# Three groups of small products in the first token mixer, written for the whole TensorE array

## The chip, the cores and the metric

The kernel runs on one core of one Trainium2 chip. The metric is device time in microseconds of one execution, as the median of several runs. Beside these runs there is one profiled execution, from which all durations below come.

## What is computed

The reference is a two-layer decoder trunk on 1024 tokens of width 1024. Layer 0 mixes tokens with RWKV-7, layer 1 with a gated DeltaNet; each is followed by a dense SwiGLU network, and by normalisations that a conditioning vector shifts and scales. Only the inner recurrence of the first mixer is touched by the change. Per head (16 heads of 64 channels) it is

```python
def step(S, inp):
    r_t, k_t, v_t, w_t, a_t, b_t = inp
    sa = jnp.einsum('bhvk,bhk->bhv', S, a_t)
    S = S * w_t[:, :, None, :] + sa[..., None] * b_t[:, :, None, :] + v_t[..., None] * k_t[:, :, None, :]
    return S, jnp.einsum('bhvk,bhk->bhv', S, r_t)
```

The kernel does this in chunks of 64 tokens: within a chunk the dependence of each step on the earlier ones is a triangular 64 by 64 system per head, whose inverse is computed with small products, and between chunks only the 64 by 64 state of each head is carried on.

## The kernel before

**Stages.** The program is written as generators that yield estimated costs, and a weaving loop (`weave`, `interleave`) that takes the next piece of whichever generator is behind. The projections of RWKV (`proj_rwkv`) come first. Then the mixer's 32 units (`pairs`: two heads, which lie in the two halves of the 128 partitions, by 256 tokens, that is four chunks) are woven with dense work: 19 of the 35 steps with the rest of the projections, the other 16 with the output projection of layer 0, its normalisation, the feed-forward of the first half of the tokens and the conditioning products of layer 1. This woven stretch goes from about 250 to 1350 us of the profile. After it come the gated DeltaNet and the rest of the dense work, in which the mixer has no part. Each engine has one queue and works it in order; what stands where in it is settled when the program is built, from the order of the code, its yields, and what each piece needs.

**A unit** has three parts.

- `prep1` makes the inputs of the four chunks. In it the scores of the two heads are computed: for each head four products of 64 rows (the head's 64 channels) by 128 columns, on one half of the array's rows (L1071), into a PSUM bank of the two under the name `p1`; then VectorE (DVE) masks them into `sa` and `sr` (L1072, L1073, whose helper has line L212) and the generator yields. The other head's four products and their two evictions follow.
- `prep2` calls `inverse` (L823 on). It works on four matrices of 128 by 128 at a time, each with two 64 by 64 blocks on its diagonal, in f16. Two of its products, the one that L895 starts (`nh` with `x`; here called the block product) and the last one, `fin` (L954: `r` with `xt`), are written as pairs of 64 by 64 products on the two diagonal quarters of the array, eight to a group. `r` comes from PSUM in one instruction on all 128 partitions: on ScalarE (ACT, L951) in the first 17 units and on DVE (L947, helper line L212) in the other 15. All products of `inverse` have line L836 and share the one PSUM bank `pa`.
- `chain` (L1112 on) carries the state through the four chunks. Per chunk: state times `ar` (L1127, 128 by 128), a subtraction-like addition on DVE (`w`), the inverse times `w` on one quarter of the array (L1136), a copy to `uv`, then the masked scores `sr` times `uv` (L1143), which add to half of the partitions of the bank `pc`, with 128 rows and 64 columns of the array, and the state's update (L1145, 128 by 128).

In the profile, the shape ahead of a matmul tells the part of the array that it uses, rows by columns: `64*128` for the scores, `64*64` for the quarters, `128*64` for L1143, `128*128` for the dense products of 512 columns (L264 to L266). A product in f32 is recorded as two matmuls, so the eight products of L1071 of a unit are 16 records and the two of L1143 in a chunk are four.

The mask of the two diagonal blocks, and the lines around the change:

```python
HALF = slice(0, 64), slice(64, P)
```

Of the kernel before, what the change touches and what calls it, by code (L numbers as in the profile page):

```python
# [10 lines left out]
F16 = mybir.dt.float16  # L11
# [4 lines left out]
ADD, SUB, MUL = ALU.add, ALU.subtract, ALU.mult  # L16

P = 128
# [39 lines left out]
def body(ctx, tc, A):  # L58
    nc = tc.nc
    pe, dve, act, pool, sync = nc.tensor, nc.vector, nc.scalar, nc.gpsimd, nc.sync  # L60
# [21 lines left out]
    def tl(pl, shape, dt, tag, bufs=1):  # L82
        return pl.tile(shape, dt, tag=tag, name=nm(tag), bufs=bufs)
# [33 lines left out]
    def p1_ps():  # L117
        return bank("p1")
# [24 lines left out]
    def C(n):  # L143
        o = COFF[n]
        return cst[:, o:o + dict(_CST)[n]]
# [65 lines left out]
    def tt(eng, out, a, b, op):  # L211
        eng.tensor_tensor(out=out, in0=a, in1=b, op=op)  # L212
# [587 lines left out]
    def setup(pl, nlev, sets):  # L800


        ms = [[tl(pl, [P, 4, P], F16, f"n{e}{q}") for e in "hl"] + [tl(pl, [P, 4, P], F16, f"nd{q}")] for q in range(2)]
        if nlev == 7:
            xt = tl(pl, [P, 4, P], F16, "xf")
        for q in range(2):
            if nlev == 7:
                ms[q].append(xt)
            for t in ms[q][3:] if nlev == 7 else ms[q][:2]:
                pool.memset(t[:, :, :], 0.0)  # L810
        zs = []
        for q in range(sets):
            zs.append([tl(pl, [P, 4, P], F16, f"z{q}{j}") for j in range(nlev - 2)])
            for z in zs[-1][:2]:
                pool.memset(z[:, :, :], 0.0)
            for z in zs[-1][2:]:
                for i in range(4):
                    act.copy(out=z[:, i, :], in_=C("ident"))
        return ms, zs

    HALF = slice(0, 64), slice(64, P)

    def inverse(pl, zs, m3, nlev, kn):  # L823


        SE, RM, FM = KN[kn]
        nh, nl, nd = m3[:3]

        def four(f, w=P):
            t = pa_ps()  # L830
            for i in range(4):
                f(t[:, w * i:w * i + w], i)
            return v3(t[:, 0:4 * w], 4)

        def one(out, l, r, start=True, stop=True):
            pe.matmul(out, l, r, start=start, stop=stop)  # L836
# [32 lines left out]
        x = series(zs[0], stack[:, 0:32].unsqueeze(1).to_broadcast([P, 4, 32]), "ix")  # L869
        xt = compact("iy")  # L870
        dve.transpose(flat(xt), flat(x))
        yield 2.0
        for m in (1, 2):
# [4 lines left out]
            if m == 1:  # L878
                xt = series(z, xt[:, :, :], "ixt")
                x = compact("iy")  # L880
# [8 lines left out]
        def half(f):  # L889
            def g(o, i):  # L890
                for R in HALF:
                    f(o[R, :], i, R)
            return g

        t = four(half(lambda o, i, R: one(o, nh[R, i, R], x[R, i, :])), 64)  # L895
        z = zs[3]
        for o in (0, 64):
            if 'z' in OP[0 if kn == 6 else 1] and o:
# [43 lines left out]
            xi = tl(pl, [P, 4, w], F16, "jxi", 1)  # L942
            tt(pool, xi[:, :, :], units, x[:, :, :], SUB)
        t = four(res, w)
        r = tl(pl, [P, 4, w], F16, "jr", 1)
        if RM == 2:
            tt(dve, r[:, :, :], t, xi[:, :, :], ADD)  # L947
        elif RM:
            tt(dve, r[:, :, :], t, units, ADD)
        else:  # L950
            act.copy(out=r[:, :, :], in_=t)  # L951
        yield 1.0

        def fin(o, i):  # L954
            if w == 64:
                for R in HALF:
                    one(o[R, :], r[R, i, :], xt[R, i, :], True, bool(FM))
            else:
                one(o, r[:, i, :], xt[:, i, :], True, bool(FM))
            if not FM:  # L960
                one(o, ident16[:, :], xt[:, i, :], False, True)

# [26 lines left out]
    def prep1(rp, nb, ctxr, h, p, q, n, box):  # L989
# [54 lines left out]
        def q4(t):  # L1044
            return t.rearrange("p (i q t) -> p i q t", i=2, q=4)
# [17 lines left out]
        yield 1.4  # L1063
        sr, sa = tl(rp, [P, 2, 2, 2, 64], F32, "sr", nb["sc"]), tl(rp, [P, 2, 2, 2, 64], F32, "sa", 1)
        inc, stc = (C("mske")[:, 64 * j:64 * j + 64].unsqueeze(1).unsqueeze(1).to_broadcast([P, 2, 2, 64]) for j in range(2))
        for hh in range(2):
            t = p1_ps()
            R = slice(64 * hh, 64 * hh + 64)
            for c in range(4):
                o = P * c  # L1070
                pe.matmul(t[:, o:o + P], bk[R, o:o + P], ar[R, o:o + P], start=True, stop=True)  # L1071
            tt(dve, sa[:, hh, :, :, :], q4(t)[:, :, 1:3, :], stc, MUL)  # L1072
            tt(dve, sr[:, hh, :, :, :], q4(t)[:, :, 0::3, :], inc, MUL)  # L1073
            yield 1.8
        m3 = ctxr[0][n % 2]
        nh, nl = m3[:2]
        for x, R in ((1, slice(0, 64)), (0, slice(64, P))):
# [34 lines left out]
    def chain(rp, nb, ctxr, h, p, q, box):  # L1112
# [7 lines left out]
        for c in range(4):  # L1120
            i, x = divmod(c, 2)
            rr, aa = (HS[0], HS[1]) if x == 0 else (HS[1], HS[0])
            np_ = tl(rp, [P, P], F32, "np", nb["np"])
            if 'n' not in OP[h]:
                act.activation(out=np_[:, :], in_=n0[:, :], func=AF.Copy, scale=dcol[:, c:c + 1])
            pq = pc_ps()
            pe.matmul(pq[:, 0:P], ar[:, P * c:P * c + P], n0[:, :], start=True, stop=True)  # L1127
            w = tl(rp, [P, P], F32, f"w{x}", 1)
            if 'w' in OP[h]:
                pe.matmul(pq[aa, 0:P], C("ident")[aa, aa], uv[aa, i, x, :], start=False, stop=True, skip_group_check=True)  # L1130
                act.copy(out=w[aa, :], in_=pq[aa, 0:P])
            else:
                tt(dve, w[aa, :], pq[aa, 0:P], uv[aa, i, x, :], ADD)
            yield 0.9
            for hs, hh in zip(HS, range(2)):
                pe.matmul(pq[aa, 128 + 64 * hh:192 + 64 * hh], tinv[aa, 2 * hh + i, :], w[aa, hs], start=True, stop=True)  # L1136
            if 'u' in OP[h]:
                act.copy(out=uv[aa, i, x, :], in_=pq[aa, P:2 * P])
            else:
                dve.tensor_copy(out=uv[aa, i, x, :], in_=pq[aa, P:2 * P])  # L1140
            yield 1.0
            for hs, hh in zip(HS, range(2)):
                pe.matmul(pq[rr, hs], sr[:, hh, i, x, :], uv[:, i, x, hs], start=False, stop=True, skip_group_check=True)  # L1143
            pst = pq[:, 2 * P:3 * P]
            pe.matmul(pst, bkn[:, c, :], uv[:, i, x, :], start=True, stop='n' not in OP[h])  # L1145
            if 'n' in OP[h]:
                pe.matmul(pst, C("ident"), n0[:, :], start=False, stop=True)
            for hs in HS:
                if 'n' in OP[h]:
                    if hs.start and 'N' in OP[h]:  # L1150
                        dve.tensor_scalar(out=n0[hs, hs], in0=pst[hs, hs], scalar1=dcol[hs, c:c + 1], scalar2=None, op0=MUL)
                    else:
                        act.activation(out=n0[hs, hs], in_=pst[hs, hs], func=AF.Copy, scale=dcol[hs, c:c + 1])
                    continue
                stt(n0[hs, hs], pst[hs, hs], dcol[hs, c:c + 1], np_[hs, hs], MUL, ADD)
            act.copy(out=yn[rr, P * i:P * i + P], in_=pq[rr, 0:P])
            yield 2.1
# [462 lines left out]
```

## Time and profile before

| what | value |
|---|---|
| median of 3 runs | 3382.88 us (3382.76 to 3385.67) |
| the profiled execution, as timed | 3386.16 us |
| its span, first to last instruction | 3384.4 us |
| mean granted TensorE clock | 0.972 |
| TensorE (PE) busy | 3222.6 us, 95% |
| DVE, ACT, POOL busy | 61%, 42%, 33% |
| window 250 to 1350 us: PE, DVE busy | 1056.94, 809.81 us |

In what follows a row of the view by groups reads: line, engine, operation, what it writes and reads, shapes, count, then the union of its busy time in us and the mean of one in ns, then idle time of its engine just before. A row of the view in order of time reads: start, duration (both us), engine, line, operation, count. The duration of a matmul in these rows reaches to its end in a pipeline, so neighbours overlap; what a matmul costs the queue is the step from its start to the start of the next.

### The profile page before, as it was taken

How to read it: one execution, taken by the hardware profiler on the slowest of the kernel's cores; microseconds unless marked ns; L12 is line 12 of the kernel's file. 1: busy time of each engine (PE TensorE's matmuls, PEld its weight loads, DVE VectorE, ACT ScalarE, POOL GpSimd, SP SyncE). 2: the span in 40 equal slices, each digit the busy share in tenths (PEclk: the TensorE clock that was granted, in tenths of full speed). 3: DMA queues.
4: the chain of work that ended last, by engine and by line, in shares of the span. 5: the costliest groups of instructions: out<-in, count | busy, mean ns of one | idle time of the engine just before them, and what ended most of it. 6: DMA issues, size and time to landing. Idle time of an engine off the chain costs nothing.

```text
span 3384.4 us, 52492 instructions
## 1 busy us (share of the span) xinstructions
PE 3222.6 (95%) x19408; PEld 2462.3 (73%) x19408; DVE 2074.1 (61%) x4534; ACT 1405.1 (42%) x2718; POOL 1129.7 (33%) x1353
## 2 busy tenths in 40 slices
PE   7989999998999999998999999999999999999997
PEld 4667777765776776676877777777777777878886
DVE  5556888887666666476476555575477653563235
ACT  4655677643333332355432232365432322342222
POOL 3553232344444443555521000220244444520001
PEclk8988999997999999999999999999999999999998
DMA  7773334352544454655654554566654446465553
GB/s 268 261 240 95 117 99 130 111 175 87 169 164 167 141 172 142 214 176 191 234 194 158 184 171 171 206 201 216 221 182 146 161 159 231 164 216 179 199 178 133
DMA packets 240529, 594.16 MB, mean 176 GB/s; under 512 B 24720, under 2 KB 80656, under 8 KB 240272
## 3 DMA queue, kind: packets, MB, share of 16 engines
q1 hardware_dynamic: 240128, 590.74, 51.8%
q8 instruction: 152, 2.49, 0.3%
q14 instruction: 105, 0.86, 0.1%
q10 hardware_dynamic: 144, 0.07, 0.0%
HBM read 440.04 MB, written 150.67 MB: 175 GB/s over the span
## 4 chain that ended last, share of the span: by engine, by line
PE 43%; DVE 4%; ACT 2%; DMA 2%; issue 2%; POOL 2%; SPq 0%; ACTq 0%; POOLq 0%; DVEq 0%
PE mm L264 13%; PE mm L265 12%; PE mm L266 12%; PE pa L836 1%; DVE e L215 1%; POOL wl L212 1%; PE p L1354 1%; DMA wr<-w_in 1%; ACT wh L222 1%; PE pc L1388 0%; PE pc L1392 0%; DMA yr<-y 0%; PE p L1336 0%; PE pc L1397 0%; PE pc L1399 0%
## 5 line engine op out<-in xcount | busy, mean ns | idle before, releaser
L264 PE MATMUL mm<-s,wh 128*128 128x512 f32 x2608 | 1079.0, 414 | 14.9 <-DVE e L215 5.5
L265 PE MATMUL mm<-s,wh 128*128 128x512 f32 x2608 | 1055.0, 405 | 11.7 <-POOL s L212 7.6
L266 PE MATMUL mm<-s,wl 128*128 128x512 f32 x2608 | 1047.8, 402 | 0.0
L212 POOL TENSOR_TENSOR wl<-wr,wh 128x256 fp32r<-128x256 f32 (+1 forms) x828 | 651.3, 817 | 876.7 <-ACT wh L222 829.4
L264 PEld LDWEIGHTS mm<-s,wh 128*128 128x128 f32 x2608 | 495.9, 190 | 132.6 <-issue 23.3
L265 PEld LDWEIGHTS mm<-s,wh 128*128 128x128 f32 x2608 | 497.2, 191 | 105.7 <-POOL s L212 12.2
L266 PEld LDWEIGHTS mm<-s,wl 128*128 128x128 f32 x2608 | 496.8, 191 | 94.8 <-POOL wl L212 0.3
L252 ACT CAST wh<-wr 128x1024 fp32r<-128x1024 f32 x199 | 206.8, 1049 | 497.8 <-PE mm L265 243.1
L222 ACT CAST wh<-wr 128x1024 fp32r<-128x1024 f32 (+1 forms) x254 | 228.4, 905 | 360.4 <-PE mm L265 196.8
L215 DVE SCALAR_TENSOR_TENSOR x<-mm,modp,x 128x512 f32<-128x512 f32 x272 | 202.3, 748 | 72.8 <-PE mm L266 70.9
L264 PE MATMUL mm<-ys,wh 128*128 128x512 f32 x544 | 219.1, 403 | 3.8 <-DVE x L215 3.8
L265 PE MATMUL mm<-ys,wh 128*128 128x512 f32 x544 | 216.9, 399 | 0.0
L266 PE MATMUL mm<-ys,wl 128*128 128x512 f32 x544 | 216.7, 398 | 0.0
L215 DVE SCALAR_TENSOR_TENSOR e<-e,vec,e 128x512 f32<-128x512 f32 x144 | 124.2, 866 | 97.2 <-ACT e L1300 89.9
L212 DVE TENSOR_TENSOR e<-mm,e 128x512 f32<-128x512 f32 x88 | 60.7, 690 | 165.2 <-PE mm L266 165.1
L836 PEld LDWEIGHTS <-z 128*128 128x128 f16 x1600 | 83.6, 97 | 100.7 <-issue 63.4
L215 DVE SCALAR_TENSOR_TENSOR e<-e,mm 128x512 f32<-128x512 f32 x88 | 60.2, 684 | 145.8 <-ACT e L679 145.5
L215 DVE SCALAR_TENSOR_TENSOR tx<-mm,modp,tx 128x512 f32<-128x512 f32 x112 | 83.1, 748 | 75.0 <-PE mm L266 73.3
L212 DVE TENSOR_TENSOR s<-e,s 128x512 fp32r<-128x512 f32 x106 | 84.1, 795 | 70.6 <-ACT s L222 70.3
L264 PEld LDWEIGHTS mm<-ys,wh 128*128 128x128 f32 x544 | 103.3, 190 | 30.5 <-DVE x L215 4.7
L266 PEld LDWEIGHTS mm<-ys,wl 128*128 128x128 f32 x544 | 103.2, 190 | 25.6
L265 PEld LDWEIGHTS mm<-ys,wh 128*128 128x128 f32 x544 | 103.4, 190 | 25.1 <-issue 0.5
(393 smaller groups left out, 5364.1 us busy)
## 6 DMA issues: line engine op xcount, KB each, us to landing
wr<-w_in SPq DMA_DIRECT2D x176, 512.0 KB, 4.5
ada<-ada_w SPq DMA_DIRECT2D x96, 512.0 KB, 5.3
loi<-wl SPq DMA_DIRECT2D x88, 512.0 KB, 2.9
wr<-w_ffo SPq DMA_DIRECT2D x88, 512.0 KB, 5.1
wl<-loi SPq DMA_DIRECT2D x88, 512.0 KB, 3.7
wr<-w_g SPq DMA_DIRECT2D x64, 512.0 KB, 4.6
lof<-wl SPq DMA_DIRECT2D x44, 512.0 KB, 2.9
wl<-lof SPq DMA_DIRECT2D x44, 512.0 KB, 3.5
```

Of the source, the lines that this page charges most:

```text
L212: eng.tensor_tensor(out=out, in0=a, in1=b, op=op)
L215: return dve.scalar_tensor_tensor(out=out, in0=a, scalar=s, in1=b, op0=op0, op1=op1)
L222: act.copy(out=hi, in_=src)
L252: act.copy(out=hi[:, :], in_=raw[:, :])
L264: pe.matmul(out, wh[:, off:off + P], ah, start=start, stop=False)
L265: pe.matmul(out, wh[:, off:off + P], al, start=False, stop=False)
L266: pe.matmul(out, wl[:, off:off + P], ah, start=False, stop=stop)
L836: pe.matmul(out, l, r, start=start, stop=stop)
L1354: pe.matmul(t[:, 256 * e:256 * e + 256], kq[:, c, 0, :], kq[:, c, :, :].rearrange("p a b -> p (a b)"), start=True, stop=True)
```

## The change

- **Scores.** Both heads' eight products are issued one after the other into two banks, then the four evictions follow, then one yield of the sum of the two earlier costs.
- **Inverse.** In the first mixer the block product and `fin` are done with four 128 by 128 products each instead of eight of 64 by 64. For this `fin` needs a left operand that is zero outside of the two diagonal blocks: a new tile `rf`, cleared once on POOL in `setup`, into whose blocks `r` is written in two instructions of 64 partitions each instead of one of 128. Of the gated DeltaNet's inverse no instruction changes.
- **Masked scores times values.** L1143 takes the scores of both chunks of the pair as its 128 columns and writes all 128 partitions of the bank, of which the half that is read is the same as before.

```diff
@@ setup
         if nlev == 7:
             xt = tl(pl, [P, 4, P], F16, "xf")
+        else:
+            rt = tl(pl, [P, 4, P], F16, "rf")
+            pool.memset(rt[:, :, :], 0.0)
         for q in range(2):
-            if nlev == 7:
-                ms[q].append(xt)
+            ms[q] += [xt if nlev == 7 else rt]
@@ inverse
-        t = four(half(lambda o, i, R: one(o, nh[R, i, R], x[R, i, :])), 64)
+        if nlev == 6:
+            t = four(lambda o, i: one(o, nh[:, i, :], x[:, i, :]), 64)
+        else:
+            t = four(half(lambda o, i, R: one(o, nh[R, i, R], x[R, i, :])), 64)
...
-        r = tl(pl, [P, 4, w], F16, "jr", 1)
-        if RM == 2:
-            tt(dve, r[:, :, :], t, xi[:, :, :], ADD)
...
-        else:
-            act.copy(out=r[:, :, :], in_=t)
+        r = m3[3] if w == 64 else tl(pl, [P, 4, w], F16, "jr", 1)
+        for R, cols in [(R, R) for R in HALF] if w == 64 else [(slice(0, P), slice(0, P))]:
+            if RM == 2:
+                tt(dve, r[R, :, cols], t[R, :, :], xi[R, :, :], ADD)
...
+            else:
+                act.copy(out=r[R, :, cols], in_=t[R, :, :])
         yield 1.0
 
         def fin(o, i):
-            if w == 64:
-                for R in HALF:
-                    one(o[R, :], r[R, i, :], xt[R, i, :], True, bool(FM))
-            else:
-                one(o, r[:, i, :], xt[:, i, :], True, bool(FM))
+            one(o, r[:, i, :], xt[:, i, :], True, bool(FM))
@@ prep1
+        both = p1_ps(), p1_ps()
         for hh in range(2):
-            t = p1_ps()
-            R = slice(64 * hh, 64 * hh + 64)
             for c in range(4):
-                o = P * c
-                pe.matmul(t[:, o:o + P], bk[R, o:o + P], ar[R, o:o + P], start=True, stop=True)
-            tt(dve, sa[:, hh, :, :, :], q4(t)[:, :, 1:3, :], stc, MUL)
-            tt(dve, sr[:, hh, :, :, :], q4(t)[:, :, 0::3, :], inc, MUL)
-            yield 1.8
+                o, R = P * c, HALF[hh]
+                pe.matmul(both[hh][:, o:o + P], bk[R, o:o + P], ar[R, o:o + P], start=True, stop=True)
+        for hh in range(2):
+            tt(dve, sa[:, hh, :, :, :], q4(both[hh])[:, :, 1:3, :], stc, MUL)
+            tt(dve, sr[:, hh, :, :, :], q4(both[hh])[:, :, 0::3, :], inc, MUL)
+        yield 3.6
@@ chain
-                pe.matmul(pq[rr, hs], sr[:, hh, i, x, :], uv[:, i, x, hs], start=False, stop=True, skip_group_check=True)
+                pe.matmul(pq[:, hs], sr[:, hh, i, :, :].rearrange("p x t -> p (x t)"), uv[:, i, x, hs], start=False, stop=True,
+                          skip_group_check=True)
```

The change also moves instructions in the queues. The first place is the scores of one unit early in the second half of the woven stretch, on PE. Before, the rows are (`p` is a scores bank, `z`, `nh` are matrices of the inverse; the last figures of a row are the partitions and elements written, and a number behind `x` counts equal rows):

```order
L836 LDWEIGHTS z_717_2344
L836 MATMUL pa_9580<-ixt_9481,z_717_2344 128x32
L1071 MATMUL p_2371_9540<-ar_9488,bk_9489 128x128 x4
L1136 MATMUL pc_9573<-w_2382_9575,ti_9311 64x64 x2
L1071 MATMUL p_2386_9593<-ar_9488,bk_9489 128x128 x4
L836 LDWEIGHTS nh_712_2335
L836 MATMUL pa_9612<-jx_9586,nh_712_2335 64x64
```

and now the same unit's scores stand like this (L1072 is L1071 of before, L1129 is L1127, L838 is L836):

```order
L265 MATMUL p_2345_9373<-l0l_2380,g2h_8543 128x256
L266 MATMUL p_2345_9373<-l0h_2379,g2l_8544 128x256
L1129 MATMUL pc_9449<-n_186_268,ar_8519 128x128
L1072 MATMUL p_2355_9406<-ar_9354,bk_9355 128x128 x4
L1072 MATMUL p_2356_9407<-ar_9354,bk_9355 128x128 x4
L838 LDWEIGHTS z_718_2346
L838 MATMUL pa_9453<-ixt_9347,z_718_2346 128x32
```

The two groups of four, which had a quarter-array product of another unit's chain between them, now stand together.

The second place is the end of a chunk in a chain, late in the stretch, also on PE, with the block product of another unit's inverse behind it. Before:

```order
L266 MATMUL mm_14898<-s_11009,wl_14890 128x512
L1143 MATMUL pc_14863<-uv_13909,sr_13798 64x64 x2
L1145 MATMUL pc_14863<-uv_13909,bkn_14022 128x128
L836 LDWEIGHTS nh_712_2335
L836 MATMUL pa_14917<-jx_14873,nh_712_2335 64x64
```

and now (L1145 is L1143 of before, L1148 is L1145):

```order
L266 MATMUL mm_14684<-s_10851,wl_14676 128x512
L1145 MATMUL pc_14656<-uv_13707,sr_13600 128x64 x2
L1148 MATMUL pc_14656<-uv_13707,bkn_13816 128x128
L838 LDWEIGHTS nh_712_2335
L838 MATMUL pa_14703<-jx_14666,nh_712_2335 128x64
```

The order is the same; the products of L1143 and of the block product write 128 partitions instead of 64, and the latter are four instead of eight. Behind the last product of the mixer PE's queue holds the same instructions in the same order as before.

More of the change, by code (lines that the diff above doesn't have):

```diff
@@ L944, in inverse @@
         t = four(res, w)
-        r = tl(pl, [P, 4, w], F16, "jr", 1)
-        if RM == 2:
-            tt(dve, r[:, :, :], t, xi[:, :, :], ADD)
-        elif RM:
-            tt(dve, r[:, :, :], t, units, ADD)
-        else:
-            act.copy(out=r[:, :, :], in_=t)
+        r = m3[3] if w == 64 else tl(pl, [P, 4, w], F16, "jr", 1)
+        for R, cols in [(R, R) for R in HALF] if w == 64 else [(slice(0, P), slice(0, P))]:
+            if RM == 2:
+                tt(dve, r[R, :, cols], t[R, :, :], xi[R, :, :], ADD)
+            elif RM:
+                tt(dve, r[R, :, cols], t[R, :, :], units[R, :, :], ADD)
+            else:
+                act.copy(out=r[R, :, cols], in_=t[R, :, :])
         yield 1.0
         def fin(o, i):
-            if w == 64:
-                for R in HALF:
-                    one(o[R, :], r[R, i, :], xt[R, i, :], True, bool(FM))
-            else:
-                one(o, r[:, i, :], xt[:, i, :], True, bool(FM))
+            one(o, r[:, i, :], xt[:, i, :], True, bool(FM))
             if not FM:
```

## The prediction

> **What bounds the kernel now.** I read the page first, for the share of each engine, then the busy times by window in the stretch where the mixer is woven with dense work, then who waited for whom there.
>
> ```profile
> span 3384.4 us, 52492 instructions
> PE 3222.6 (95%) x19408; PEld 2462.3 (73%) x19408; DVE 2074.1 (61%) x4534; ACT 1405.1 (42%) x2718; POOL 1129.7 (33%) x1353
> PE 43%; DVE 4%; ACT 2%; DMA 2%; issue 2%; POOL 2%; SPq 0%; ACTq 0%; POOLq 0%; DVEq 0%
> ```
>
> PE is the engine that is nearly always at work, and the chain that ended last lies mostly on it. By window of 50 us (length, then busy us of PE, weight loads, DVE, ACT, POOL, then the granted clock), with the sum over all 22 windows from 250 to 1350 us last:
>
> ```profile
> 400.00:450.00 50.00, 49.97 (x475) 37.55 (x472) 44.66 (x132) 36.52 (x98) 16.00 (x21) 1.00 0.38 118
> 550.00:600.00 50.00, 49.36 (x448) 37.08 (x447) 44.70 (x123) 38.69 (x99) 14.54 (x21) 1.00 0.48 149
> sum 1100.00, PE 1056.94 PEld 774.99 DVE 809.81 ACT 535.60 POOL 438.42; mean PE 48.04 PEld 35.23 DVE 36.81 ACT 24.35 POOL 19.93
> ```
>
> PE is idle for 43 of 1100 us there. The next engine is DVE, at 89% in the fullest windows. PE's own waits in the stretch (us in total, times, longest) are few, and mostly for DVE:
>
> ```profile
> PE pa L836 <- DVE ixt L212: 8.7, 8, 3.0
> PE pa L836 <- DVE z L876: 5.6, 5, 2.3
> PE pc L1136 <- DVE w L212: 4.7, 5, 1.8
> PE pa L836 <- ACT jr L951: 0.3, 1, 0.3
> ```
>
> So what PE's queue is relieved of in this stretch shortens the time, as long as the other engines keep up. Behind it nothing changes.
>
> **The price of leaving the whole array.** Busy time hides it; the steps between starts show it. Here is the end of a chunk in a chain, from the view in order of time (start, duration):
>
> ```profile
> 1009.25 0.40 PE L265 MATMUL mm<-s,wh 128*128 128x512 f32 x1
> 1009.48 0.39 PE L266 MATMUL mm<-s,wl 128*128 128x512 f32 x1
> 1009.80 0.45 PE L1143 MATMUL pc<-uv,sr 128*64 128x64 f32 x4
> 1010.17 0.49 PE L1145 MATMUL pc<-uv,bkn 128*128 128x128 f32 x2
> 1010.59 0.31 PE L836 MATMUL pa<-jx,nh 64*64 64x64 f16 x8
> ...
> 1024.30 0.39 PE L1127 MATMUL pc<-n,ar 128*128 128x128 f32 x2
> 1024.53 0.26 PE L836 MATMUL pa<-stack,z 128*128 128x32 f16 x4
> ```
>
> A dense product takes a step of 0.23 us (1009.25 to 1009.48), but the one ahead of L1143 takes 0.32: entering another part of the array costs 0.09. Two records of a 128 by 128 product take 0.23 in peace (1024.30 to 1024.53), but 0.42 at L1145, with a change of tile on both sides. Of the 0.19 more, 0.09 is the next change; the other 0.10 is its weight load, which could not be done ahead. Every change of tile thus costs 0.09, and the first f32 product behind it 0.10 more.
>
> **Masked scores times values.** Before: 0.09 to enter, 0.37 for L1143 with its exit, 0.42 - 0.09 = 0.33 for L1145, together 0.79. Now there is no change, L1145 takes 0.23, and four records of 64 moving columns go through the whole array. The trace has none of that shape; its neighbours are 128 moving columns, above (0.115 each), and 32 moving columns:
>
> ```profile
> 1501.62 0.39 PE L1257 MATMUL mm<-g_g,cst 128*128 128x32 f32 x2
> 1501.84 0.47 PE L264 MATMUL mm<-s,wh 128*128 128x512 f32 x1
> ```
>
> Two of these take 0.22, or 0.11 each, so the price lies between 0.11 and 0.115 and I take 0.112: 4 x 0.112 + 0.23 = 0.68. That saves 0.11 a chunk (0.10 to 0.12), and 128 chunks (512 records, below) give 14 us.
>
> ```profile
> L1143 PE MATMUL pc<-uv,sr 128*64 128x64 f32 x512 | 58.8, 239 | 0.5 <-DVE uv L1140 0.5
> L836 PE MATMUL pa<-jxt,jr 64*64 64x64 f16 x256 | 10.0, 198 | 0.3 <-ACT jr L951 0.3
> ```
>
> **Block product and `fin`.** A group of eight quarter-array products between dense ones, and single products of the shape that takes their place:
>
> ```profile
> 1020.57 0.47 PE L264 MATMUL mm<-s,wh 128*128 128x512 f32 x1
> 1020.98 0.31 PE L836 MATMUL pa<-jxt,jr 64*64 64x64 f16 x8
> 1021.22 0.50 PE L265 MATMUL mm<-s,wh 128*128 128x512 f32 x1
> 1021.55 0.40 PE L266 MATMUL mm<-s,wl 128*128 128x512 f32 x1
> ...
> 1019.43 0.19 PE L836 MATMUL pa<-jx,nh 128*128 128x64 f16 x1
> 1019.46 0.19 PE L836 MATMUL pa<-jx,nl 128*128 128x64 f16 x1
> ```
>
> Before: 0.09 to enter, 0.24 with the exit, and 0.10 more for the dense product behind (0.33 instead of 0.23), 0.43 in all. Now: four times 0.03, or 0.12. That saves 0.31, and the two products of 32 units are 64 groups (256 records of eight each, twice): 20 us. The Trainium skill speaks against this edit: its page TensorEngine Tiling (Array Packing), section Theoretical Speedup, has small dimensions of up to 64 gain up to two times per dimension from tiles that work side by side. By that page the whole array would take back up to half of the products' speed, which I estimate as 64 groups of 0.12 us more, 8 us, and the sum would be smaller by that. The rows do not bear it out: the eight tiled products took 0.24 - 0.09 = 0.15 us without their exit, four whole ones take 0.12.
>
> **Scores.** A group of four in the middle of dense work:
>
> ```profile
> 999.74 1.16 PE L1071 MATMUL p<-ar,bk 64*128 64x128 f32 x8
> 1000.83 0.50 PE L264 MATMUL mm<-s,wh 128*128 128x512 f32 x1
> 1001.16 0.40 PE L265 MATMUL mm<-s,wh 128*128 128x512 f32 x1
> ```
>
> Eight records take 1.09 us and the next product 0.33. At 0.112 a record 0.90 would do, so such a trip costs 0.09 in, 0.19 for first load and exit, 0.10 behind: 0.38. I counted the trips in the two orders of PE's queue: PE goes to this tile 68 times before and 45 times now, since the two heads' groups now mostly stand together. 23 x 0.38 gives 9 us.
>
> **What the three share.** The savings overlap where two tiled pieces stood side by side and shared a change: of such places the order has 72 before and 17 now, so 55 changes were counted twice, at 0.09 + 0.10 each: 10 us. 14 + 20 + 9 - 10 leaves 33; counted the other way, the changes of tile fall from 1097 to 726, 371 x 0.09 = 33 us, with 371 loads of 0.10 in f32 and less in f16, about 26 us, less 512 x (0.112 - 0.059) = 27 us for L1143's longer records (0.059 is what its records cost inside 128*64: 0.37 less exit and first load, over four). That leaves 32, which I take.
>
> **What is added.** `r` is written by two instructions instead of one, and scores are evicted four in a row:
>
> ```profile
> L951 ACT CAST jr<-pa 128x256 f16<-128x256 f32 x17 | 6.2, 366 | 2.1 <-PE pa L836 1.9
> L212 DVE TENSOR_TENSOR jr<-pa,jxi 128x256 f16<-128x256 f32 x15 | 6.3, 419 | 7.3 <-PE pa L836 4.1 <-POOL jxi L212 2.5
> L212 DVE TENSOR_TENSOR sa<-p,cst 128x256 f32<-128x256 f32 x64 | 27.0, 421 | 22.7 <-PE p L1071 22.2
> L212 DVE TENSOR_TENSOR sr<-p,cst 128x256 f32<-128x256 f32 x64 | 26.4, 412 | 0.0
> L810 POOL MEMSET nh<- 128x512 f16 x2 | 1.1, 525 | 0.0
> ```
>
> As the columns per partition stay, I price the second write of `r` like the first: 17 x 0.37 + 15 x 0.42 = 12.6 us on ACT and DVE. It is hidden by PE's dense products, and delays only `fin`. PE's wait for `jr` was 0.3 us in all, so I take 2 us of it; the bounds are 0 and 12.6, if each unit waited it out. The clearing of `rf`, like the others of 0.5 us, stands on POOL before the mixer's first product, beside RWKV's projections; I take 0, and 0.5 if POOL's next split of a weight is late by it. The four evictions keep DVE for 1.67 us in a row instead of twice 0.83, with `w` and `uv` of other units' chains queued behind, for which L1136 and L1143 wait; this and shorter work between a product and the one that needs its result make PE wait more. I take 5 us more than the 43, from a bound of -5 (later yields could also fit better) to 15 (a third more).
>
> The sum against the profiled execution: 3386.16 - 32 + 2 + 5 = 3361.2 us. The median of the runs lies 3.28 us under that execution, so the forecast is 3358 us.
>
> **Rivals.**
>
> *DVE sets the pace.* At 44.7 of 50 us, with 3% less time for the same work and more of it, DVE could hold the chains up where it is fullest, until 700 us, where about half of the units lie. Then half of the 32 is lost and 7 us stay as waits: 3382.9 - 16 + 7 = 3374. For it speaks that PE's waits are for DVE; against it, that PE was idle for 0.03 us in the window from 400 with DVE at 89%.
>
> *The clock.* PE pays for a cluster of waits with half speed:
>
> ```profile
> 775.00:800.00 25.00, 19.13 (x191) 12.66 (x189) 20.08 (x59) 9.92 (x23) 8.10 (x11) 0.88 0.32 105
> 800.00:825.00 25.00, 21.77 (x76) 13.92 (x76) 19.95 (x47) 11.77 (x22) 10.73 (x15) 0.50 0.10 32
> 825.00:850.00 25.00, 24.96 (x160) 17.96 (x159) 14.23 (x45) 9.56 (x21) 9.50 (x14) 0.80 0.34 111
> ...
> 801.82 0.63 PE L266 MATMUL mm<-s,wl 128*128 128x512 f32 x1
> 802.25 0.63 PE L264 MATMUL mm<-s,wh 128*128 128x512 f32 x1
> ```
>
> Read as half or full, the three clocks give 6 + 25 + 10 = 41 us at half speed, where a step takes 0.43 instead of 0.23, so 41 x 0.47 = 19 us are lost. If the changed order fills this place, the time is 3358 - 19 = 3339. The same can happen elsewhere with the other sign. The Trainium skill's page TensorE: Matmul & The Clock Gate, section Part 1, has the gate at half or full alone and opened by about 3.4 us of sustained work; by that rule it can go either way here, and the 0.50 agrees with it.
>
> *Slower: the scores' banks.* Two banks are held at once, until DVE has emptied them in 4 x 0.42 = 1.67 us. If PE's next product that needs one of them stands right behind, PE, which works in order, waits: 32 x 1.67 = 53 us, and 3358 + 53 = 3411. It decides from 25 / 32 = 0.8 us per unit on. For it: DVE is so full that its evictions queue. Against it: in the order the next user of such a bank (the transposes of L1087) mostly has other products ahead of it, and needs only the first bank, free after half of that time.
>
> *The change doesn't do what it says,* if the 0.09 and 0.10 came from something else than the change of tile. Then L1143 alone counts, 27 us: 3410. The steps speak against it, as they are the same beside three kinds of tiled products.
>
> **How the numbers follow.** 0.68 for the forecast, whose own range is 3346 to 3370 (the bounds of `r` and of the waits); 0.13 for DVE, 0.11 for the clock, 0.05 for the banks, 0.03 for the last. The range 3338 to 3377 takes in the forecast, the clock and DVE's case. A measurement of this kernel can tell 0.2%, or 6.8 us, from no change, so faster is under 3376.1: the forecast, the clock and half of DVE's case, 0.86; the same is the other half, 0.06; slower 0.08.
>
> **What would show it.** Right: the tiled shapes 128*64 and, in the stretch, 64*64 of L836 are gone; L1143's records step by 0.11 us without 0.09 ahead; the stretch to the mixer's last product is shorter by some 25 us and all behind it is as long as before. Wrong: PE's idle time in the stretch well over 48 us, waits for `sa` and `sr` or for `rf` in the list, or half-speed stretches at other places.

## The result and the profile after

The changed kernel took 3352.0 us (median of 4 runs, 3345.24 to 3356.1) beside 3383.57 us for the kernel before on the same chip (4 runs, 3382.76 to 3385.67). The ratio is 0.991, with a 95% interval from 0.9894 to 0.9926. The forecast was 3358 us. The profiled execution took 3354.26 us.

The head of the page of after, with the same columns as before:

```profile
span 3352.5 us, 52022 instructions
PE 3190.3 (95%) x19152; PEld 2460.3 (73%) x19152; DVE 2083.6 (62%) x4549; ACT 1410.7 (42%) x2735; POOL 1134.6 (34%) x1354
```

PE has 256 products fewer and is busy for 32 us less; it is still the engine that sets the time. To see where the 31.9 us of the span went, I cut both traces at the first scores product and at the mixer's last transposes (L1181 before, L1184 after). The busy times by window, before first (length, then busy us and count of PE, weight loads, DVE, ACT and POOL, the granted clock, the DMA share, GB/s):

```profile
0.00:255.40 255.40, 219.27 (x1010) 147.93 (x1010) 133.41 (x232) 141.72 (x251) 122.19 (x162) 0.93 0.76 256
255.40:1357.00 1101.60, 1059.36 (x8391) 777.20 (x8391) 812.12 (x2199) 535.70 (x1285) 433.49 (x566) 0.97 0.42 135
1357.00:3384.40 2027.40, 1943.94 (x10011) 1537.21 (x10009) 1128.60 (x2104) 727.71 (x1183) 574.03 (x625) 0.98 0.55 187
```

The same of after:

```profile
0.00:249.40 249.40, 216.04 (x1010) 146.27 (x1010) 133.32 (x232) 141.83 (x251) 123.64 (x163) 0.94 0.77 263
249.40:1327.10 1077.70, 1032.50 (x8135) 778.19 (x8135) 822.83 (x2214) 540.49 (x1302) 435.64 (x566) 0.97 0.43 138
1327.10:3352.50 2025.40, 1941.78 (x10011) 1535.88 (x10009) 1127.42 (x2104) 728.38 (x1183) 575.36 (x625) 0.98 0.55 187
```

The woven stretch is 23.9 us shorter, what lies behind it 2.0 us. The other 6.0 us lie ahead of the first scores product, where PE's count is the same (1010) and the clock 0.94 instead of 0.93. The change edits nothing there but one clearing on POOL, and in the eight later profiles of kernels that contain the change this product starts anywhere from 249.0 to 254.2 us: most of these 6.0 us belong to the run.

PE in order of time, at the end of a chunk in a chain and at a `fin` (start, duration):

```profile
987.09 0.40 PE L266 MATMUL mm<-s,wl 128*128 128x512 f32 x1
987.33 0.55 PE L1145 MATMUL pc<-uv,sr 128*128 128x64 f32 x4
987.72 0.44 PE L1148 MATMUL pc<-uv,bkn 128*128 128x128 f32 x2
987.99 0.28 PE L838 MATMUL pa<-jx,nh 128*128 128x64 f16 x4
988.11 0.42 PE L1089 MATMUL p<-cst,ld 128*128 128x128 f32 x2
...
998.31 0.40 PE L265 MATMUL mm<-s,wh 128*128 128x512 f32 x1
998.54 0.29 PE L838 MATMUL pa<-jxt,rf 128*128 128x64 f16 x4
998.67 0.47 PE L266 MATMUL mm<-s,wl 128*128 128x512 f32 x1
998.99 0.39 PE L264 MATMUL mm<-s,wh 128*128 128x512 f32 x1
```

The 0.09 ahead of L1145 is gone (987.09 to 987.33 is a dense step of 0.24), and L1145 with L1148 takes 0.66 us where 0.68 was forecast. The block product takes 0.12 (987.99 to 988.11), as forecast. But the dense product behind `fin` still takes 0.32 (998.67 to 998.99) and not 0.23, although no tile is changed there any more. That term of the prediction was mis-sized, as is told below.

PE's waits in the stretch (us, times, longest), and the tile that is new:

```profile
PE pa L838 <- DVE z L878: 6.7, 7, 2.4
PE pc L1138 <- DVE w L212: 6.5, 8, 1.6
PE pa L838 <- DVE ixt L212: 5.9, 4, 2.3
PE p L1072 <- DVE yo L212: 2.1, 3, 1.1
PE pa L838 <- ACT rf L957: 1.3, 3, 0.5
PE p L1072 <- DVE bv L212: 0.4, 1, 0.4
PE pa L838 <- DVE rf L212: 0.2, 1, 0.2
```

```profile
L957 ACT CAST rf<-pa x34: 348/367/368, 272.1 to 658.8; 64x256 f16<-64x256 f32 x34
L212 DVE TENSOR_TENSOR rf<-pa,jxi x30: 403/423/428, 694.0 to 1296.5; 64x256 f16<-64x256 f32 x30
L808 POOL MEMSET rf<- x1: 519/519/519, 231.7 to 231.7; 128x512 f16 x1
```

Half the partitions cost the same time in the writing of `r` (367 and 423 ns, as 366 and 419 before), as was assumed; the wait for it is 1.5 us instead of 0.3.

**How the stretch is divided below.** For each PE record I took the time to the start of the next. Records with the same neighbours (tile, moving columns, type and output of the record ahead, the record and the one behind) form a group over all fourteen profiles, and the lowest quarter of a group's steps is taken as what the step costs when nothing is waited for. The sum of these is "PE's own steps", which include changes of tile and weight loads that are not hidden. What goes beyond it at full clock is waits; the rest lies in the parts at half clock.

| stretch, us | length | PE's own steps | waits | lost at half clock | changes of tile in it |
|---|---|---|---|---|---|
| before | 1101.6 | 980.7 | 85.8 | 35.2 | 905 |
| after | 1077.7 | 959.6 | 89.5 | 28.7 | 534 |

So of the 23.9 us, 21.1 are PE's own steps and 6.5 the clock, while 3.7 came back as waits (11 if only waits of over 60 ns are added up: 67.7 and 78.8). The division is no sharper than its groups: drawn in other ways, they give 18 to 24 us for PE's own steps and 3 to 8 for the waits that came back. And in a second profile of the changed kernel, the run change_again below, the same queue has 4 to 7 us less of waits than here, about as many as before. So the fall of PE's own steps is clear, and the rise of the waits is not.

### The profile page after: what moved, and what is told of

It reads as the page before. It is cut to its first block, busy times and chain, and to the rows that moved or that the text cites. A ratio compares the mean times of both kernels' runs of the same rounds, so it can differ in the third digit from the quotient of the medians.

```text
span 3352.5 us, 52022 instructions
## 1 busy us (share of the span) xinstructions
PE 3190.3 (95%) x19152; PEld 2460.3 (73%) x19152; DVE 2083.6 (62%) x4549; ACT 1410.7 (42%) x2735; POOL 1134.6 (34%) x1354
## 5 line engine op out<-in xcount | busy, mean ns | idle before, releaser
L264 PE MATMUL mm<-s,wh 128*128 128x512 f32 x2608 | 1076.3, 413 | 14.8 <-DVE e L215 5.4
L264 PEld LDWEIGHTS mm<-s,wh 128*128 128x128 f32 x2608 | 494.7, 190 | 134.2 <-issue 24.8
L264 PE MATMUL mm<-ys,wh 128*128 128x512 f32 x544 | 219.8, 404 | 5.8 <-DVE x L215 5.8
L838 PEld LDWEIGHTS <-z 128*128 128x128 f16 x1600 | 85.2, 98 | 97.9 <-issue 59.2
L215 DVE SCALAR_TENSOR_TENSOR tx<-mm,modp,tx 128x512 f32<-128x512 f32 x112 | 83.2, 748 | 79.0 <-PE mm L266 78.8
L264 PEld LDWEIGHTS mm<-ys,wh 128*128 128x128 f32 x544 | 103.9, 191 | 32.6 <-DVE x L215 6.6
```

What stands on the lines that cost most here:

```text
L215: return dve.scalar_tensor_tensor(out=out, in0=a, scalar=s, in1=b, op0=op0, op1=op1)
L264: pe.matmul(out, wh[:, off:off + P], ah, start=start, stop=False)
```

## The experiments

The theory was the prediction's: what counts is how often PE changes the tile. The rivals were that fewer instructions on PE make the gain, that the scores' shorter order of evictions and the merged yield do, or that the two banks held at once cost something. Each ratio is to the kernel before on the same chip. The profiles of one kernel differ in their clock, and so do the times, so the table after the experiments also gives each at equal clock.

**The three parts alone.** The first has only L1143's whole-array form in the kernel before:

```diff
-                pe.matmul(pq[rr, hs], sr[:, hh, i, x, :], uv[:, i, x, hs], start=False, stop=True, skip_group_check=True)
+                pe.matmul(pq[:, hs], sr[:, hh, i, :, :].rearrange("p x t -> p (x t)"), uv[:, i, x, hs], start=False, stop=True,
+                          skip_group_check=True)
```

> Of the change only the masked scores times values go to the whole array. Theory (every change of the array's tile costs 0.09 us and the first f32 product behind it 0.10 more): PE's order has 866 changes of tile instead of 1097, worth about 38 us, less 27 us for L1143's longer records, so 11 us faster than before (3372), with steps of 0.112 us between L1143's records. Rival (the time goes with the number of PE instructions, not with tiles): no instruction goes and the records get longer, so 0 to 27 us slower. Rival (the single yield of the scores and its evictions made the gain): no difference from before.

Measured: 3367.79 us (3356.64 to 3376.08, 8 runs) beside 3379.48; ratio 0.9965 [0.995, 0.9981]. It is faster with not one PE instruction fewer and with longer records, which ends the rival of the instruction count. The group of the new records, with the mean ns of one:

```profile
L1145 PE MATMUL pc<-uv,sr 128*128 128x64 f32 x512 | 78.3, 275 | 1.0 <-DVE uv L1142 0.5 <-ACT uv L1140 0.2
```

This row is of after. Busy time alone would have said the opposite of the truth: 78.3 us instead of 58.8. The step from one such record to the next is 112 ns (median of 242 in the stretch), as assumed.

The second has only the scores' edit (both heads' products, then the four evictions, one yield):

```diff
+        both = p1_ps(), p1_ps()
         for hh in range(2):
...
+        yield 3.6
```

> Of the change only the two heads' scores are issued in one go. Theory of tiles: 1084 changes of tile instead of 1097, about 3 us faster, hardly to be told from no change; the prediction's term of 9 us for the scores would be too large, since it counted trips to this tile alone and not the others that came with the new order. Rival (the yield and the evictions carry the gain): 20 to 30 us faster. Rival (the two banks are held too long): slower by up to 53 us, with PE waiting for DVE's sa and sr.

Measured: 3378.72 us (12 runs) beside 3379.48; 0.9999 [0.9982, 1.0016]. The changes of tile in the stretch fell from 905 to 892 only. There is no slowdown from the two banks either.

The third has only the inverse's edit (`rf`, the block product and `fin` on the whole array):

```diff
...
-            if w == 64:
-                for R in HALF:
-                    one(o[R, :], r[R, i, :], xt[R, i, :], True, bool(FM))
...
+            one(o, r[:, i, :], xt[:, i, :], True, bool(FM))
```

> Of the change only the block product and the last product of the inverse go to the whole array, with r written in two instructions. Theory of tiles: 992 changes of tile instead of 1097, about 16 us faster than before (3368), less a few us if r is waited for. Rival (number of PE instructions): the whole gain of about 30 us, since only here instructions go. Rival (small tiles side by side are faster): about 8 us slower than the theory of tiles has it.

Measured: 3372.52 us (12 runs); 0.9983 [0.997, 0.9995]. That is 6 us by the ratio, and 11.5 at equal clock, about half of the 20 us that the prediction gave it.

**The change without its scores' part,** which stands as before:

```diff
-        both = p1_ps(), p1_ps()
+            t = p1_ps()
...
+            yield 1.8
```

> The change without its scores, which are issued as before. Theory of tiles: 742 changes of tile instead of the change's 726, so 29 us faster than before (3354), within 3 us of the full change. Rival (yield and evictions carry it): most of the gain is gone. If the two parts alone give 11 and 16 us and this gives about 29, the parts add up.

Measured: 3365.76 us (7 runs); 0.9953 [0.9937, 0.997]. That is about half of the 29 us that the expectation had. By the medians it is less than the change; at equal clock, 16.5 us, it can't be told from it. With the run of the scores alone: the scores' part is worth 0 to 3 us. PE's own steps of the other two parts add up (8.0 and 9.3, together 18.4; table below), their times at equal clock less so (10.6 and 11.5, together 16.5), at the edge of what can be told.

**A change of tile by itself.** Two kernels add one small f16 product, whose result nothing reads, to each chunk, ahead of L1129's. In the first it lies on a quarter of the array, in the second on the whole:

```diff
+            pe.matmul(pq[0:64, 3 * P:3 * P + 32], ident16[0:64, 0:64], ident16[0:64, 0:32], start=True, stop=True)
```

> The changed kernel, with one more product per chunk of each chain (128 in all) ahead of L1129: 64 by 64 of the identity with 32 columns in f16 on a quarter of the array, into a part of the bank that nobody reads. Theory of tiles: 937 changes of tile instead of 726, about 32 us slower than the changed kernel, as slow as before (3383). Rival (the number of instructions counts): 128 small products of 0.03 us, 4 us slower than the changed kernel.

```diff
+            pe.matmul(pq[:, 3 * P:3 * P + 32], ident16[:, :], ident16[:, 0:32], start=True, stop=True)
```

> The same as the trip to a quarter of the array, but the extra product uses the whole array (128 by 128, 32 columns, f16), so nothing is left but its own time. Theory of tiles: 717 changes of tile, as in the changed kernel, so 0 to 4 us slower than it (3352 to 3356). Rival (any small product between the dense ones costs what the trip costs): as slow as with the quarter-array product.

Measured: 3366.16 us, 0.9965 [0.9947, 0.9982], and 3361.25 us, 0.9948 [0.9928, 0.9967] (11 runs each, beside 3380.93). The same place in order of time, tiled first:

```profile
987.93 0.26 PE L838 MATMUL pa<-iy,nd 128*128 128x32 f16 x4
988.13 0.20 PE L1129 MATMUL pc<-ident 64*64 64x32 f16 x1
988.26 0.49 PE L1130 MATMUL pc<-n,ar 128*128 128x128 f32 x2
988.50 0.47 PE L264 MATMUL mm<-s,wh 128*128 128x512 f32 x1
```

```profile
993.32 0.27 PE L838 MATMUL pa<-iy,nd 128*128 128x32 f16 x4
993.43 0.18 PE L1129 MATMUL pc<-ident 128*128 128x32 f16 x1
993.45 0.47 PE L1130 MATMUL pc<-n,ar 128*128 128x128 f32 x2
993.68 0.48 PE L264 MATMUL mm<-s,wh 128*128 128x512 f32 x1
```

From the first start to L264 it is 0.57 us with the trip and 0.36 without: 0.09 more ahead of the small product and 0.11 more behind it, on the way back. The price of a change is there. At equal clock (table below) the tiled trips bring the kernel back to the time of before, +1.2 ± 1.8 us, as expected; the trips on the whole array leave it 10.4 us faster than before, 6 to 7 us slower than the change, where 0 to 4 were expected. So the two kernels lie 11.6 us apart at equal clock and 4.9 by the medians, far less than the 27 to 31 of the expectations. One cause is in the trace: the expectations laid the late load behind each trip to the change of tile, but behind a short f16 product it is late in both kernels. The 220 changes between the two (745 and 525 in the stretch) at 0.09 us make 20 us, and PE's own steps differ by 18.2; where the other 7 us went is not shown. The clocks differ too, for the tiled one ran higher:

```profile
core 0: 3366.1 us, clock 0.980
```

```profile
core 0: 3368.3 us, clock 0.973
```

The Trainium skill's page TensorEngine Tiling (Array Packing), section Key Properties, has a change of the tiling mode drain the TensorE. The trace agrees that such a change costs time, and puts the price at 0.09 us.

**Eight products, but on the whole array.** Block product and `fin` are issued twice each, so that PE has as many instructions there as before:

```diff
-            t = four(lambda o, i: one(o, nh[:, i, :], x[:, i, :]), 64)
+            t = four(lambda o, i: [one(o, nh[:, i, :], x[:, i, :]) for _ in HALF], 64)
...
-            one(o, r[:, i, :], xt[:, i, :], True, bool(FM))
+            for _ in HALF if w == 64 else (0,):
+                one(o, r[:, i, :], xt[:, i, :], True, bool(FM))
```

> The changed kernel, but the block product and the last product of the inverse are issued twice each on the whole array, eight instead of four per group, so that PE has as many instructions as before the change. Theory of tiles: 719 changes of tile, 256 products of 0.03 us more, so 6 to 8 us slower than the changed kernel and still about 25 us faster than before. Rival (the number of instructions counts): the gain of the inverse's part is gone, 16 to 30 us slower than the changed kernel.

Measured: 3365.76 us (12 runs); 0.9951 [0.9936, 0.9965]. Still clearly faster than before, and behind the change by about 256 products of 0.03 us, or 8 us: the changed kernel, run again further down, has 0.9928, which is 7.8 us less.

**The inverse times the right side too.** L1138, the last tiled product in a chain, is done on the whole array, with zeros beside its blocks, and `ti` is written by two DVE instructions. The cleared `w` tiles are shared by all units, so neighbouring chains overwrite each other's `w` and the output is not the reference's.

```diff
-                pe.matmul(pq[aa, 128 + 64 * hh:192 + 64 * hh], tinv[aa, 2 * hh + i, :], w[aa, hs], start=True, stop=True)
+                pe.matmul(pq[:, 128 + 64 * hh:192 + 64 * hh], tinv[:, 2 * hh + i, :], w[:, hs], start=True, stop=True)
```

> The changed kernel, and the inverse times w (L1138, the last product of the chain on a quarter of the array) on the whole array too: the inverse is written into a cleared tile of 128 columns in two instructions of 64 partitions, and w into a tile whose other half is zero. Theory of tiles: 506 changes of tile instead of 726, worth 35 us, less 27 us for records of 0.112 instead of 0.058 us, so about 8 us faster than the changed kernel (3344), less what the longer step and 32 more DVE instructions of 0.42 us cost the chain. Rival (DVE sets the pace by now): no faster, or slower by up to 13 us.

Measured: 3367.5 us (12 runs); 0.9959 [0.9943, 0.9975], which misses the expectation: it is not faster than the change. The changes of tile went on falling, to 314 in the stretch, and yet the stretch is 7 us longer than in after (1085 and 1078 us). By the division above, PE's own steps fell by 8.3 us and the waits grew by 14.6; but the new records stand in this one kernel alone, and by most other ways to draw the groups the waits grow by 0 to 7 us only. The view of waits has PE stand 9.5 us for `w` (there `wf`) where it stood 6.5 in after. The second write of `ti`, and `w` tiles that are held in common, are both in this; which of them it is was not tried apart.

**Work taken from the mixer, and from the dense side.** Both begin from the changed kernel, which ran again beside them. The first leaves out L1145's products:

```diff
-            for hs, hh in zip(HS, range(2)):
-                pe.matmul(pq[:, hs], sr[:, hh, i, :, :].rearrange("p x t -> p (x t)"), uv[:, i, x, hs], start=False, stop=True,
-                          skip_group_check=True)
```

> The changed kernel without the masked scores times values (the product of L1145 is left out, so the output lacks that term). It takes 57 us of matmul steps (512 records of 0.112) from PE's queue, on the mixer's side, without lengthening anything. Theory of a queue that is PE's alone: 57 us faster than the changed kernel. Theory that below about 975 us of PE's own work in the stretch most of what is taken away comes back as waits for the mixer's results: 10 to 30 us faster.

The second leaves out one of three products of a dense projection:

```diff
+        if not light:
+            pe.matmul(out, wh[:, off:off + P], ah, start=start, stop=False)
-        pe.matmul(out, wh[:, off:off + P], al, start=False, stop=False)
+        pe.matmul(out, wh[:, off:off + P], al, start=start and light, stop=False)
...
+                mm3(ps[:, :], w, P * k, u[k], k == 0, k == KT - 1, (l, h, j) == (0, 0, 1))
```

> The changed kernel with the first of the three products left out in the second half of the feed-forward's input weights of layer 0, first tokens (22 tiles of 8 products of 0.228 us: 40 us of PE's work; the output is then not the reference's). All on the dense side, in the second half of the stretch; no product of the mixer changes. Theory of PE's queue: 40 us faster than the changed kernel. Theory that the mixer's own chain of results paces the stretch by now: 20 us or less.

> The changed kernel itself, timed again beside the kernel before on this chip, since the first comparison had four runs a side and the single runs of one kernel here differ by up to 25 us along with the mean granted clock (0.971 to 0.981). If the first comparison stands, 31 us faster than before (ratio 0.991). If the parts tell more (all but the scores: ratio 0.9953), 14 to 20 us faster, and the rest of the first difference was the clock.

Measured, beside 3378.74: without the masked product 3337.59 us (5 runs), 0.9874 [0.985, 0.9899]; with less dense work 3330.03 us (4 runs), 0.9848 [0.9829, 0.9867]; the change again 3357.22 us (5 runs), 0.9928 [0.991, 0.9946]. The change again lies between the two values that its expectation named; at equal clock its 17.7 us are what the parts tell, and the rest of the first difference is the clock.

Against the change in the same stretch, 54 us of PE's own steps went in the first and 32 in the second (144 of its 176 products lie in it). At equal clock the first gave 32 us and the second 34, by the medians 20 and 27. Of the 40 us of dense work that was taken away most comes back: the stretch is 30 to 34 us shorter than in the two profiles of the change. Of the mixer's 54 us a good part does not, and there are more waits for the mixer's own results. Those of the kernel without the masked product:

```profile
PE pa L838 <- DVE ixt L212: 9.6, 7, 3.7
PE pa L838 <- DVE z L878: 8.1, 7, 2.8
PE pc L1138 <- DVE w L212: 7.7, 7, 3.7
PE pc L1129 <- DVE n L215: 3.8, 7, 0.7
PE pa L838 <- ACT rf L957: 3.1, 6, 0.8
```

They are waits that after has too, each longer here. The reading that fits: a chain's products follow each other through DVE, and with less PE work between them PE comes too early.

**The scores with the heads in turn:**

```diff
-        for hh in range(2):
-            for c in range(4):
+        for c in range(4):
+            for hh in range(2):
```

> The changed kernel with the two heads' scores issued in turn, head by head for each of the four products, instead of four and four. In the trace of the changed kernel the second head's weight load and product start within 4 ns of the first head's where the groups meet: the two halves of the array's rows work side by side. If that holds all along, 16 records of a unit take 8 steps of 0.112 instead of 16, 0.9 us less a unit, 29 us of PE's work less, and the time falls by 10 to 29 us below the changed kernel, depending on how much comes back as waits. If the halves overlap only where the groups meet, no difference.

Measured: 3360.66 us (6 runs); 0.9934 [0.9914, 0.9955], the same as the change, and not the 10 to 29 us faster that were expected of halves that overlap all along. What it showed of the hardware stands at the end.

All runs in one table. "At equal clock" comes from a fit over the runs of all kernels: a value for each kernel, and one slope for the mean granted clock of the run, which came out at -2.5 us for each 0.001, with a scatter of 2.4 us about it; ± is a 95% interval. The runs of before in it are the 70 of the three later sets, since the first set's have no clock on record. The last two columns are differences to before.

| kernel | ratio | at equal clock, us | PE's own steps in the stretch, us |
|---|---|---|---|
| change | 0.991, again 0.9928 | -16.4 ± 2.6, -17.7 ± 2.2 | -21.1 |
| sr_only | 0.9965 | -10.6 ± 1.8 | -8.0 |
| inverse_only | 0.9983 | -11.5 ± 1.5 | -9.3 |
| scores_only | 0.9999 | -1.0 ± 1.5 | -1.7 |
| all_but_scores | 0.9953 | -16.5 ± 1.9 | -18.4 |
| scores_alternating | 0.9934 | -14.9 ± 2.1 | -20.9 |
| trip_tiled | 0.9965 | +1.2 ± 1.8 | +6.5 |
| trip_whole | 0.9948 | -10.4 ± 1.6 | -11.7 |
| eight_whole | 0.9951 | -10.1 ± 1.5 | -16.5 |
| inverse_times_whole | 0.9959 | -11.6 ± 1.5 | -29.4 |
| no_masked_product | 0.9874 | -48.8 ± 2.3 | -75.2 |
| lighter_dense | 0.9848 | -50.7 ± 2.5 | -53.1 |

The two columns come from different things, the one from all runs' times, the other from steps in a single profile. They agree within some 6 us, but for inverse_times_whole and no_masked_product. Another way to draw the groups moves the last column by 1 to 4 us in most rows, by 6 for trip_tiled and by 8 for inverse_times_whole.

## Why the prediction was right, and where it was not

**The total.** Forecast 3358, measured 3352.0 and later 0.9928 of before, which is 3358.5 on the 3382.88 us that the forecast began from. The nearness of the total is worth less than it seems, because two terms were too large, and the clock gave something that was not in the forecast: at equal clock the change is worth 16 to 18 us, where the forecast had 25. That the sum came out so near is in part luck. The forecast's own range has a slip as well: with its bounds of 12.6 us for `r` and 15 for the waits its upper end is 3379 and not 3370.

**The changes of tile: right.** 1097 and 726 were read from the order; the traces have exactly these counts, and 0.09 us each stands in the trip experiment too. The rival that the change doesn't do what it says has fallen.

**Masked scores times values: right.** 0.66 us a chunk at the place above, 0.68 forecast, 14 us in all; the part alone gave 12 us by the medians and 10.6 at equal clock. Alone it takes out 231 changes of tile and not two for each of 128 chunks; 25 x 0.09 is 2 us less.

**Block product and `fin`: mis-sized, 20 us where about 14 was to be had.** The mis-sized term is "0.10 more for the dense product behind", which the prediction laid to the change of tile. The dense product behind four whole-array f16 products also takes 314 ns (median of 23 places behind `rf`) instead of about 230; behind the eight tiled ones it took 336. So of the 0.31 us a group, 0.09 stays, and 64 x 0.22 gives 14. Alone the part takes out 105 changes of tile and not 128, another 2 us less, which makes 12 beside the 11.5 at equal clock. It could have been seen in the trace of before, behind other f16 groups on the whole array:

```profile
1026.40 0.27 PE L836 MATMUL pa<-ix,z 128*128 128x32 f16 x4
1026.51 0.48 PE L264 MATMUL mm<-s,wh 128*128 128x512 f32 x1
1026.83 0.39 PE L265 MATMUL mm<-s,wh 128*128 128x512 f32 x1
```

0.11 for the group, and then 0.32 for a dense product that takes 0.23 elsewhere. The places where f16 is followed by f32 on the whole array rise from 231 to 337 in the stretch; 106 x 0.085 is 9 us, which turns the 32 of the sum into 23, beside the 21.1 that the steps show. That the cause is the f32 weight load, for which a short product ahead leaves no time, fits the records of the loads: in after, the load for the dense product behind `rf` starts at 998.65, 0.03 us ahead of its product, and the one for the next dense product at 998.76, 0.23 us ahead. It was not tried by itself.

**The scores: mis-sized, 9 us where 0 to 3 came.** 23 trips fewer were counted on the order, but what counts is the changes of tile of the whole queue, and these fell by 13 with this part alone and by 16 with it on top of the others (742 to 726): where the two groups came together, other tiled products came to stand alone.

**The waits: 7 us forecast, 4 to 11 more in one profile, about none in the other.** PE's idle time in the stretch went from 42 to 45 us. That the waits would be for DVE's results is borne out, the 2 us for `rf` too (1.5), but the 5 us beside it can't be told from the spread of two profiles. The risk lies further on: without the masked product, waits take 26 us more than in after (115.1 instead of 89.5; 16 to 26 by the way the groups are drawn), and PE is idle for 65 us.

**The rivals.** DVE as the pace: not in this change, where DVE is busy for 822.8 of 1077.7 us, 76% where it was 74%, and 3.7 us of waits were added and not 16. Beyond it PE waits more for DVE's results, though without the masked product DVE is busy for only 822 of 1060 us. The clock: 6.5 us less were lost at half clock in the stretch. But the place that the rival named was not filled: half clock from 797 us on lasted for 37.5 us before, and in the second profile of the changed kernel it lasts for as long from 768 us on. So what the clock gave was luck of the run, as far as the two profiles tell. The banks: 2.5 us of waits of L1072's products for `yo` and `bv`, where 53 us were at stake, and no slowdown with that part alone.

## What to carry to other kernels

Where one engine is busy without a break, cost an edit by the steps from start to start, with the product behind included, and look for the same neighbour without the edit: the late start that seems to belong to a change of tile may be there anyway. Count such changes over the engine's whole queue and not for the operation that is edited. And ask of each microsecond taken from a chain of dependent products whether there is other work to fill it: beyond the change, dense work taken away came back for the most part here (34 of 40 us), work of the chains to a smaller part (32 of 54).

## What the hardware showed besides

**Row halves run side by side where the two heads' products stand close in the queue.** The scores' products lie on 64 of the 128 rows each, one head on either half. The changed kernel, run again, with sixteen records in a row, where one head's eight stand ahead of the other's:

```profile
473.69 1.71 PE L1073 MATMUL p<-ar,bk 64*128 64x128 f32 x16
475.33 0.29 PE L839 MATMUL pa<-jx,nh 128*128 128x64 f16 x4
```

and the kernel with the heads in turn, at a place where the records start 6 to 8 and 104 to 106 ns behind each other in turn:

```profile
1073.08 1.16 PE L1072 MATMUL p<-ar,bk 64*128 64x128 f32 x16
1074.17 0.27 PE L838 MATMUL pa<-iy,nd 128*128 128x32 f16 x4
```

Sixteen records take 1.09 us there and 1.64 above, where only those around the meeting of the two groups overlap. Eight records of one head by themselves took 1.09 us before (999.74 to 1000.83, shown in the prediction). The Trainium skill's page TensorEngine Tiling (Array Packing), section Theoretical Speedup, has a small dimension of up to 64 gain up to two times. The trace agrees for f32 on row halves, and by the full factor: sixteen in the time of eight. It brought nothing here, since the build put most of the products back, wholly or partly, into groups of one head: short and long steps take turns all along in five of the 32 units only, and 95 steps in the stretch are under 60 ns, where after has 56.

**The time of a run follows its clock.** Of one set of 26, single runs of the kernel before lie between 3364.52 us at a mean granted clock of 0.980 and 3390.33 at 0.971: a spread of 0.8%, as much as the whole change. The changed kernel's runs had 0.979 in the first measurement and 0.976 in the second, beside 0.974 for before. Whether the change raises the clock or the runs fell so stays open: with 4 and 5 runs it can't be told.
